# Eight of the 22 up-projection pairs of a ConvFFN computed as seven quarter products instead of eight, with the weight sums on GpSimd

## The chip, the cores and the metric

The kernel runs on one core of one Trainium2 chip. The metric is device microseconds of one execution, and the number for a kernel is the median over its runs. Five engines work side by side, each through its own queue of instructions in order: TensorE (PE in the profile) multiplies matrices, VectorE (DVE), ScalarE (ACT) and GpSimd (POOL) do elementwise work, and SyncE (SP) issues transfers; GpSimd issues some transfers as well. An instruction that waits for another engine holds back all that stands behind it in its own queue.

## The reference

One decoder layer on 512 tokens of width 1024: three token mixers, a gated merge, an output projection, and then the part that the change touches, a gated feed-forward net with a causal convolution over time:

```python
h = rmsnorm(x, norm_ffn_pre)                  # 512 x 1024
u = h @ ffn_w_up                              # 512 x 5632: gate and value halves
u = causal_conv3(u) + b                       # depthwise, over time
y = gelu_tanh(u[:, :2816]) * u[:, 2816:]      # 512 x 2816
x = x + rmsnorm(y @ ffn_w_down, norm_ffn_post)
```

The names in these lines are shortened; the arithmetic is float32.

## The kernel before

**Precision.** Every float32 operand of a matmul is split in two: `hi`, a rounded copy in TensorE's float32 format (made by ScalarE), and `lo`, the rest (a subtraction on VectorE). A product is then three matmuls, hi·hi, lo·hi and hi·lo, added up in PSUM. `mm3` (lines 112 to 114) issues them for the projections. `split` (lines 70 and 71) makes the hi and lo of a weight tile: one cast of 128x1024 on ScalarE, one subtraction of 128x1024 on VectorE.

**Weights of the up-projection.** `ffn_w_up` lies in memory as 44 tiles of 128x1024, one tile for each 128 output channels: eight blocks of 128 columns, one for each 128 of the 1024 input channels. Tile 2n is the gate half of pair n and tile 2n+1 its value half, so there are 22 pairs. `load_raw` loads a tile (line 66, on SP's queue, two buffers tagged `raw`), `split` makes `whi` and `wlo` (four buffers each), and `weight` keeps two tiles ahead of the one in use.

**The up stage.** The normalised tokens stand transposed as `h2h` and `h2l` (eight blocks of 128 channels by 512 tokens). For each tile the eight blocks are multiplied and added up in one PSUM tile of 128 channels x 512 tokens: 8 x 3 = 24 matmuls of 128x512, 48 for a pair. Pairs 0 and 1 (`FIRST`) are done as two halves of 256 tokens each while the tokens are still being made. `conv` (lines 838 to 841) is one ScalarE pass and two VectorE passes over the PSUM tile, and `up_finish` applies GELU (line 853), multiplies the halves of the pair (lines 855 and 863) and prepares operands for the down stage: even pairs make `y7` and one part of `ay`, odd pairs three sums in `ay` (lines 856 to 867, 128x256 each, on VectorE).

**The down stage** is already made of seven products where the plain way takes eight: tokens, output columns and the 22 input blocks are halved, and `steps` lists for each of the seven the left operand (a sum of halves of y) and the weight quarter that is added to or loaded into the chain of weights. `chain_load` (lines 879 to 886) does that with transfers: SP's queue loads a quarter, GpSimd's queue (line 884) adds one in flight. `l_split` (lines 933 and 934) makes hi and lo of a left operand, four blocks at a time, in two `lhs` buffers; step 0 takes `y7`, which is ready made. `q_mm` (lines 963 to 965) issues 462 matmuls of 128x512 in all.

**What sets the order.** The program is written in the order of its stages, and a scheduler places each engine's instructions; on TensorE the order is that of the program. Buffers with tags go round, so an early load waits until the last reader of its buffer is done.

Of the kernel before, what the change touches and what calls it, by code (L numbers as in the profile page):

```python
# [52 lines left out]
def kernel(ctx: ExitStack, tc: tile.TileContext, x, xT, w_first, w_tiles, w_v, w_br, w_out, w_up, w_down,  # L53
# [776 lines left out]
    with tc.tile_pool(name="fp", bufs=1) as fp:  # L830
        y7 = fp.tile([P, 2, NH, TH], F32R, tag="y7", name="y7")
        a2 = fp.tile([P, 2, NH, TH], F32, tag="a2", name="a2")
        ay = fp.tile([P, 4, NH, TH], F32, tag="ay", name="ay")
# [11 lines left out]
        kept = {}  # L845

        def up_finish(n, pg, pv):

# [4 lines left out]
            nc.scalar.activation(tg, tg, AF.Gelu_apprx_tanh)
            if n % 2 == 0:
                nc.vector.tensor_mul(tg, tg, tv)
                nc.vector.tensor_sub(tv[:, :TH], tg[:, TH:], tg[:, :TH])
                nc.scalar.copy(y7[:, 0, i, :], tv[:, :TH])
                nc.scalar.copy(ay[:, 2, i, :], tg[:, :TH])
                nc.vector.tensor_sub(y7[:, 1, i, :], tv[:, :TH], y7[:, 0, i, :].bitcast(F32))
                kept[i] = tg  # L860
            else:
# [1 line left out]
                nc.vector.tensor_mul(a2[:, :, i, :], tg.rearrange("p (h t) -> p h t", h=2),
                                     tv.rearrange("p (h t) -> p h t", h=2))
# [2 lines left out]
                nc.vector.tensor_sub(ay[:, 3, i, :], a2[:, 0, i, :], ay[:, 1, i, :])
# [262 lines left out]
```

## Time and profile before

| | us |
|---|---|
| median of 3 runs (lowest to highest) | 779.81 (779.64 to 779.97) |
| the profiled execution, its own time | 779.64 |
| span of the profile | 777.9 |
| up stage, matmuls from 423.8 to 666.5 | 242.7 |
| of this pairs 2 to 21, from 448.85 to 666.47 | 217.6 |
| down stage, from 666.5 to the last matmul's start at 771.0 | 104.5 |

The profile is of one execution. Its span starts with the first instruction and ends with the last; 1.7 us of the execution's own time lie around it. The granted clock of TensorE was 0.999 of full speed. A row of a group names the line of the kernel, the engine and the operation, `out<-in` by the program's names without buffer numbers, the shape and the count; behind the bar stand busy time, mean ns of one, and the idle time of the engine just before. A row of the timeline begins with start and duration. Matmuls overlap: the next starts before the last has ended, so the distance between two starts, not the duration, tells what one costs.

### The profile page before, as it was taken

What the parts mean: (1) busy time and instruction counts of PE and PEld (TensorE: products, weight loads), DVE (VectorE), ACT (ScalarE), POOL (GpSimd) and SP (SyncE); (2) the same over time, 40 slices, a digit from 0 to 9 for tenths busy, and PEclk for the clock granted to TensorE, in tenths of its full rate; (3) what the DMA queues carried; (4) which work ended last, traced back from release to release, by engine and by line L of the source; (5) the groups of instructions that cost most, each with busy time, mean ns of one, the idle gap of its engine ahead of it and who ended that gap; (6) DMA issues with size and microseconds to landing.
All of it is one profiled execution on the core that took longest, in us unless ns stands there. A gap on an engine that the chain in (4) does not pass through costs nothing.

```text
span 777.9 us, 9728 instructions
## 1 busy us (share of the span) xinstructions
PE 769.8 (99%) x3686; PEld 639.0 (82%) x3686; DVE 514.6 (66%) x784; ACT 357.0 (46%) x583; POOL 55.7 (7%) x70
## 2 busy tenths in 40 slices
PE   9999999999999999999999999999999999999996
PEld 7899776888887887888888988888888888888885
DVE  5564678378696557654748557766666666766896
ACT  6554554482223342432535434434444343565582
POOL 0100000002503000000000100000000000233000
PEclk9999999999999999999999999999999999999999
DMA  8524212123134222232461473332322325499761
GB/s 308 189 94 146 71 56 81 55 82 109 54 98 133 82 81 72 92 109 81 136 217 54 142 211 109 109 108 82 110 90 100 107 83 136 130 187 194 195 214 54
DMA packets 28527, 92.56 MB, mean 119 GB/s; under 512 B 3393, under 2 KB 3665, under 8 KB 28481
## 3 DMA queue, kind: packets, MB, share of 16 engines
q1 hardware_dynamic: 24048, 77.83, 29.8%
q0 software_dynamic: 4288, 14.11, 9.2%
q8 instruction: 29, 0.48, 0.2%
q14 instruction: 18, 0.14, 0.1%
q10 hardware_dynamic: 144, 0.00, 0.0%
HBM read 89.84 MB, written 2.10 MB: 118 GB/s over the span
## 4 chain that ended last, share of the span: by engine, by line
PE 98%; DVE 0%; DMA 0%; issue 0%; ACT 0%; DVEq 0%
PE up L113 10%; PE up L114 10%; PE up L112 10%; PE pj L112 9%; PE pj L113 9%; PE pj L114 9%; PE q L965 4%; PE q L964 4%; PE q L963 4%; PE py L114 3%; PE py L113 3%; PE py L112 3%; PE pq L206 3%; PE pz L752 2%; PE pz L750 2%; PE pz L751 2%
## 5 line engine op out<-in xcount | busy, mean ns | idle before, releaser
L71 DVE TENSOR_TENSOR wlo<-raw,whi 128x1024 fp32r<-128x1024 f32 (+1 forms) x105 | 125.4, 1196 | 110.7 <-ACT whi L70 110.4
L70 ACT CAST whi<-raw 128x1024 fp32r<-128x1024 f32 (+1 forms) x105 | 107.4, 1025 | 184.4 <-PE pj L113 92.5
L112 PE MATMUL up<-h_hi,whi 128*128 128x512 f32 (+1 forms) x384 | 143.8, 375 | 0.0
L113 PE MATMUL up<-h_lo,whi 128*128 128x512 f32 (+1 forms) x384 | 142.8, 372 | 0.0
L114 PE MATMUL up<-h_hi,wlo 128*128 128x512 f32 (+1 forms) x384 | 142.5, 371 | 0.0
L112 PE MATMUL pj<-h_hi,whi 128*128 128x512 f32 x296 | 120.8, 408 | 0.0
L113 PE MATMUL pj<-h_lo,whi 128*128 128x512 f32 x296 | 116.1, 392 | 0.0
L114 PE MATMUL pj<-h_hi,wlo 128*128 128x512 f32 x296 | 115.8, 391 | 0.0
L113 PEld LDWEIGHTS up<-h_lo,whi 128*128 128x128 f32 x384 | 72.3, 188 | 12.6
L114 PEld LDWEIGHTS up<-h_hi,wlo 128*128 128x128 f32 x384 | 72.3, 188 | 12.5
L112 PEld LDWEIGHTS up<-h_hi,whi 128*128 128x128 f32 x384 | 72.2, 188 | 12.3
L112 PEld LDWEIGHTS pj<-h_hi,whi 128*128 128x128 f32 x296 | 55.7, 188 | 16.2 <-issue 3.4
L114 PEld LDWEIGHTS pj<-h_hi,wlo 128*128 128x128 f32 x296 | 55.6, 188 | 12.0 <-issue 0.2
L113 PEld LDWEIGHTS pj<-h_lo,whi 128*128 128x128 f32 x296 | 55.8, 188 | 10.7 <-issue 1.2
L71 DVE TENSOR_TENSOR wlo<-chain,whi 128x1024 fp32r<-128x1024 f32 (+1 forms) x42 | 47.3, 1131 | 20.0 <-ACT whi L70 20.0
L70 ACT CAST whi<-chain 128x1024 fp32r<-128x1024 f32 (+1 forms) x42 | 41.2, 981 | 29.6 <-PE q L965 22.7
L884 POOL DMA_DIRECT2D chain<-in_w_down_dram x24 | 21.1, 878 | 435.1 <-DMA chain<-in_w_down_dram 200.0
L963 PE MATMUL q<-whi,lhs 128*128 128x512 f32 x132 | 51.3, 389 | 0.0
L964 PE MATMUL q<-wlo,lhs 128*128 128x512 f32 x132 | 51.3, 389 | 0.0
L965 PE MATMUL q<-whi,lhs 128*128 128x512 f32 x132 | 51.3, 389 | 0.0
L675 DVE TENSOR_TENSOR g<-pj,rstd_b 128x512 f32<-128x512 f32 x24 | 16.4, 687 | 27.3 <-PE pj L114 27.3
L963 PEld LDWEIGHTS q<-whi,lhs 128*128 128x128 f32 x132 | 24.8, 188 | 5.2
(308 smaller groups left out, 1264.8 us busy)
## 6 DMA issues: line engine op xcount, KB each, us to landing
raw<-in_w_up_dram SPq DMA_DIRECT2D x44, 512.0 KB, 3.3
raw<-in_w_tiles_dram SPq DMA_DIRECT2D x37, 512.0 KB, 3.3
chain<-in_w_down_dram SPq DMA_DIRECT2D x20, 512.0 KB, 4.5
chain<-in_w_down_dram POOLq DMA_DIRECT2D x20, 512.0 KB, 6.9
raw<-in_w_br_dram SPq DMA_DIRECT2D x12, 512.0 KB, 3.3
raw<-in_w_out_dram SPq DMA_DIRECT2D x8, 512.0 KB, 3.3
raw<-in_w_v_dram SPq DMA_DIRECT2D x8, 328.0 KB, 3.0
xT<-in_xT_dram SPq DMA_DIRECT2D x8, 256.0 KB, 5.1
```

What stands on the lines that cost most here:

```text
L70: nc.scalar.copy(hi[:, c], raw[:, c])
L71: nc.vector.tensor_sub(lo[:, c], raw[:, c], hi[:, c].bitcast(F32))
L112: nc.tensor.matmul(ps, lh, rh, start=first, stop=False)
L113: nc.tensor.matmul(ps, lh, rl, start=False, stop=False)
L114: nc.tensor.matmul(ps, ll, rh, start=False, stop=last)
L206: nc.tensor.matmul(pq[i], w[:, kc, i * P : (i + 1) * P], h[:, kc, :], start=kc == 0 and n == 0, stop=kc == KC - 1 and n == 2)
L675: nc.vector.tensor_mul(g1, gates.pop((br, m)), rstd_b)
L750: nc.tensor.matmul(pz[t][n], mh[:, kc % 4, tk], wh[:, ns], start=kc == 0, stop=False)
L884: nc.gpsimd.dma_start(c, w_down[kh, nh, :, k, :], accum_op=ALU.add)
L963: nc.tensor.matmul(ps, hi, wh[:, c], start=k == 0 and not last, stop=False, skip_group_check=last)
L964: nc.tensor.matmul(ps, hi, wl[:, c], start=False, stop=False, skip_group_check=last)
L965: nc.tensor.matmul(ps, lo, wh[:, c], start=False, stop=k == NH - 1, skip_group_check=last)
```

## The change

`SEVEN` lists eight pairs, 5, 7, ... 19. Each is done together with the plain pair behind it.

For such a pair the gate tile and the value tile are taken as one matrix with four quarters: b11 and b21 are the gate tile's columns for the first and the second half of the input channels, b12 and b22 those of the value tile. The tokens are halved too. Seven products of quarters (each 4 blocks x 3 = 12 matmuls of 128 channels x 256 tokens, line 1047) take the place of the eight plain ones: 84 matmuls of 128x256 for 48 of 128x512. Four of the seven take sums of quarters of the tokens as moving operand: `ys[0]` to `ys[3]`, made once by `y_steps` on VectorE and ScalarE during pairs 2 to 4, in five parts. Four take sums of weight quarters: `p3 = b12 + b22`, `p2 = b11 + p3`, `p1 = b11 + b12`, `p4 = b21 + p2`, added by GpSimd (lines 927 to 929 and 948) from two raw tiles `sra` and `srb` that `s_load` loads while the pair before is in work. `half` splits a quarter of 128x512 into hi and lo.

TensorE's order for two pairs n and n+1 is: b11, b21, p3, six matmuls of the plain tile 2n+2, p2, nine of it, p1, nine of it, p4, b22, and then the 24 of tile 2n+3. p2, p1 and b22 add to the PSUM tile `bx` in which b11 stands. `keep` copies the state of it between them to SBUF on ScalarE (`q1`, `nv`, `u`, and `n7` of p3), since the next product writes over it. Three VectorE operations (lines 1078, 1091, 1092) and one copy (line 1094) put the gate's and the value's result together in `ua` and `ub`, and `up_finish` goes on from SBUF.

The ring of weights is now made of half tiles (`slots`), in the same four buffers; `fill` prepares as many items ahead as fit.

`up_finish` writes one tensor `act`; of the sums for the down stage it makes one per pair, on GpSimd (lines 902 and 904), and the others are made by `l_split` in the down stage, in place, on VectorE (lines 1021 and 1023). Step 0 of the down stage has no ready operand any more, so `l_split` runs for it as well. The `lhs` buffers lie where `ys[2]` and `ys[3]` were, and four of the six chain buffers where `ys[0]` and `ys[1]` were, so that the chain loads follow the last of the eight pairs.

```diff
+SEVEN = (5, 7, 9, 11, 13, 15, 17, 19)
...
-        y7 = fp.tile([P, 2, NH, TH], F32R, tag="y7", name="y7")
-        a2 = fp.tile([P, 2, NH, TH], F32, tag="a2", name="a2")
-        ay = fp.tile([P, 4, NH, TH], F32, tag="ay", name="ay")
-        ch = [fp.tile([P, 2 * T], F32, tag=f"ch{p}", name=f"chain{p}") for p in range(4)]
+        act = fp.tile([P, 5, NH, TH], F32, tag="act", name="act")
+        wt = [new_w() for _ in range(4)]
...
+            whole(t1, 0, 1)
+            whole(t2, 1, 1)
+            nc.vector.tensor_sub(t2, t2, t1)
+            yield
+            parts(2, t2)
...
             if n % 2 == 0:
-                nc.vector.tensor_mul(tg, tg, tv)
-                nc.vector.tensor_sub(tv[:, :TH], tg[:, TH:], tg[:, :TH])
-                nc.scalar.copy(y7[:, 0, i, :], tv[:, :TH])
-                nc.scalar.copy(ay[:, 2, i, :], tg[:, :TH])
-                nc.vector.tensor_sub(y7[:, 1, i, :], tv[:, :TH], y7[:, 0, i, :].bitcast(F32))
-                kept[i] = tg
+                nc.gpsimd.tensor_sub(act[:, 4, i, :], act[:, 1, i, :], act[:, 0, i, :])
             else:
-                t0 = kept.pop(i)
-                nc.vector.tensor_mul(a2[:, :, i, :], tg.rearrange("p (h t) -> p h t", h=2),
-                                     tv.rearrange("p (h t) -> p h t", h=2))
-                nc.vector.tensor_sub(ay[:, 0, i, :], t0[:, TH:], a2[:, 1, i, :])
-                nc.vector.tensor_sub(ay[:, 1, i, :], t0[:, :TH], ay[:, 0, i, :])
-                nc.vector.tensor_sub(ay[:, 3, i, :], a2[:, 0, i, :], ay[:, 1, i, :])
+                nc.gpsimd.tensor_sub(act[:, 1, i, :], act[:, 1, i, :], act[:, 3, i, :])
...
+            for j, g in enumerate(("sra", "srb")):
+                qt[g] = f4(f"{g}{n}", g)
+                nc.sync.dma_start(qt[g], w_up[2 * n + j])
+            a, b = qt["sra"], qt["srb"]
...
+            nc.gpsimd.tensor_add(qt["p3"], b[:, :T], b[:, T:])
+            nc.gpsimd.tensor_add(qt["p2"], a[:, :T], qt["p3"])
+            nc.gpsimd.tensor_add(qt["p1"], a[:, :T], b[:, :T])
...
+            if q == "b21":
+                r = half(a[:, T:])
+                nc.gpsimd.tensor_add(a[:, T:], a[:, T:], qt["p2"])
+                return r
+            if q == "b22":
+                r = half(b[:, T:])
+                later = [m for m in SEVEN if m > n]
+                if later:
+                    s_load(later[0])
+                return r
...
+            quarter(bx, "b11", hq(0, 0), True)
+            q1 = keep("q1", bx)
+            quarter(bz, "b21", hq(1, 0), True)
+            nc.vector.tensor_add(ua[:, :TH], bz[:, :TH], q1)
+            quarter(by, "p3", yq(0), True)
+            n7 = keep("n7", by)
+            w = up_weight("t", 2 * n + 2)
+            whole_mm(pn[0], w, range(0, 2))
+            quarter(bx, "p2", yq(1), False)
+            nv = keep("nv", bx)
+            whole_mm(pn[0], w, range(2, 5))
+            quarter(bx, "p1", yq(2), False)
+            u = keep("u", bx, -1.0)
+            whole_mm(pn[0], w, range(5, 8))
...
+            quarter(by, "p4", hq(1, 1), False)
+            nc.vector.tensor_add(ua[:, TH:], by[:, :TH], nv)
+            nc.vector.tensor_sub(ub[:, TH:], u, n7)
+            quarter(bx, "b22", yq(3), False)
+            nc.scalar.activation(ub[:, :TH], bx[:, :TH], AF.Copy, scale=-1.0)
+            up_finish(n, ua, ub)
+            whole_mm(pn[1], up_weight("t", 2 * n + 3), range(KC))
...
+            if s == 3:
+                nc.vector.tensor_sub(src, src, act[:, 1, k0:k1, :])
+            if s == 5:
+                nc.vector.tensor_sub(src, act[:, 2, k0:k1, :], act[:, 0, k0:k1, :])
```

**How the order of the engines moves.** ScalarE in the up stage, before: the casts of two pairs' four weight tiles (line 70) with the work of `up_finish` between them.

```order
L70 CAST whi_4713<-raw_4711 128x1024
L838 ACTIVATE t0_4698<-up26_4642,small_sb_86 128x512
L853 ACTIVATE t0_4698<-t0_4698 128x512
L70 CAST whi_4744<-raw_4742 128x1024
L838 ACTIVATE t0_4702<-up27_4673,small_sb_86 128x512
L70 CAST whi_4789<-raw_4787 128x1024
L838 ACTIVATE tk_4773<-up28_4717,small_sb_86 128x512
L853 ACTIVATE tk_4773<-tk_4773 128x512
L70 CAST whi_4820<-raw_4818 128x1024
```

ScalarE now, from the first copy of pair 15 on (line 1068 is `keep`, line 933 the cast in `half`, line 941 the cast of a whole tile, names that end in `_15` and `_17` belong to these pairs):

```order
L1068 ACTIVATE q1_5091<-ux_15_5068 128x256
L933 CAST whi_3664<-sra15_4904 128x512
L933 CAST whi_3664<-srb15_4906 128x512
L941 CAST whi_3666<-raw_5134 128x1024
L1068 ACTIVATE n7_5132<-uy_15_5069 128x256
L1068 ACTIVATE nv_5156<-ux_15_5068 128x256
L933 CAST whi_3668<-sra17_5110 128x512
L933 CAST whi_3670<-p3_17_5116 128x512
L1068 ACTIVATE u_5179<-ux_15_5068 128x256
L933 CAST whi_3668<-sra17_5110 128x512
L884 ACTIVATE t0_5224<-ua_15_5073,small_sb_86 128x512
```

The copy `u` of pair 15 now stands behind two casts for pair 17, and these read what a load (`sra17`) and a GpSimd sum of a second load (`p3_17`) bring.

VectorE at the same place, before, for one pair:

```order
L71 TENSOR_TENSOR wlo_4714<-raw_4711,whi_4713 128x1024
L839 SCALAR_TENSOR_TENSOR t0_4698<-up26_4642,small_sb_86,t0_4698 128x511
L841 SCALAR_TENSOR_TENSOR t0_4698<-up26_4642,small_sb_86,t0_4698 128x510
L71 TENSOR_TENSOR wlo_4745<-raw_4742,whi_4744 128x1024
L839 SCALAR_TENSOR_TENSOR t0_4702<-up27_4673,small_sb_86,t0_4702 128x511
L841 SCALAR_TENSOR_TENSOR t0_4702<-up27_4673,small_sb_86,t0_4702 128x510
L863 TENSOR_TENSOR a2_3676<-t0_4698,t0_4702 128x2x256
L865 TENSOR_TENSOR ay_3677<-tk_4622,a2_3676 128x256
L866 TENSOR_TENSOR ay_3677<-tk_4622,ay_3677 128x256
L867 TENSOR_TENSOR ay_3677<-a2_3676,ay_3677 128x256
```

VectorE now, from the product of pair 15's halves to the last subtraction of pair 17's weights (lines 934 and 942 are the subtractions for quarters and whole tiles):

```order
L899 TENSOR_TENSOR act_3663<-t0_5224,t0_5228 128x2x256
L887 SCALAR_TENSOR_TENSOR t0_5263<-up32_5071,small_sb_86,t0_5263 128x510
L934 TENSOR_TENSOR wlo_3667<-p2_17_5115,whi_3666 128x512
L934 TENSOR_TENSOR wlo_3667<-p1_17_5114,whi_3666 128x512
L885 SCALAR_TENSOR_TENSOR t0_5267<-up33_5072,small_sb_86,t0_5267 128x511
L934 TENSOR_TENSOR wlo_3669<-sra17_5110,whi_3668 128x512
L887 SCALAR_TENSOR_TENSOR t0_5267<-up33_5072,small_sb_86,t0_5267 128x510
L1078 TENSOR_TENSOR ua_17_5279<-uz_17_5276,q1_5297 128x256
L899 TENSOR_TENSOR act_3663<-t0_5263,t0_5267 128x2x256
L934 TENSOR_TENSOR wlo_3669<-srb17_5112,whi_3668 128x512
L942 TENSOR_TENSOR wlo_3671<-raw_5340,whi_3670 128x1024
```

The three sums of 128x256 per pair have gone from here to GpSimd and into the down stage; the subtraction on `srb17`, after which the buffer `srb` may be loaded for pair 19, stands next to last in this stretch, behind two convolutions.

ScalarE at the end of the up stage, now, in pair 19 and the tiles 42 and 43 of pair 21 (`raw_5592`, `raw_5596`; `chain01` is a chain buffer of the down stage, line 1024 the cast in `l_split`):

```order
L1068 ACTIVATE u_5581<-ux_19_5480 128x256
L941 CAST whi_3670<-raw_5596 128x1024
L1024 CAST lhs2_5733<-act_3663 128x1024
L941 CAST whi_3668<-raw_5592 128x1024
L71 CAST whi_3664<-chain01_5673 128x1024
L1094 ACTIVATE ub_19_5486<-ux_19_5480 128x256
L884 ACTIVATE t0_5627<-ua_19_5485,small_sb_86 128x512
L884 ACTIVATE t0_5631<-ub_19_5486,small_sb_86 128x512
```

Before, the chains were loaded at the start of the up stage, and each chain's cast stood behind the convolution of the tile whose buffer it took; now the cast of the first chain stands ahead of pair 19's last copy out of PSUM.

More of the change, by code (lines that the diff above doesn't have):

```diff
@@ new lines, in half, with prep @@
+        def half(src):
+            hi, lo = slots(1)
+            nc.scalar.copy(hi, src)
+            nc.vector.tensor_sub(lo, src, hi.bitcast(F32))
+            return hi, lo
+        def prep(item):
+            if item[0] == "t":
+                hi, lo = slots(2)
+                raw = load_raw(w_up[item[1]])
+                nc.scalar.copy(hi, raw)
+                nc.vector.tensor_sub(lo, raw, hi.bitcast(F32))
+                return hi, lo
+            n, q = item[1:]
+            a, b = qt["sra"], qt["srb"]
+            if q == "b21":
[8 more added lines that the diff above has]
+                return r
+            return half(a[:, :T] if q == "b11" else a[:, T:] if q == "p4" else qt[q])
@@ new lines, with fill, up_weight @@
+        place = {}
+        def fill():
+            while done["i"] < len(items):
+                it = items[done["i"]]
+                size = 2 if it[0] == "t" else 1
+                at = slot["n"] + (size == 2 and slot["n"] % 2)
+                if at + size - min(place.values(), default=at) > 8 or (it[0] == "s" and not qt):
+                    break
+                place[it] = at
+                got_w[it] = prep(it)
+                done["i"] += 1
+        def up_weight(*item):
+            assert items[done["taken"]] == item, (items[done["taken"]], item)
+            done["taken"] += 1
+            fill()
+            return got_w[item]
@@ L873, with free @@
+        def free(*item):
+            del place[item]
+        steps = ((act[:, 4], (1, 1), True), (act[:, 0], (0, 0), False), (act[:, 1], (0, 1), True),
+                 (act[:, 0], (1, 1), True), (act[:, 3], (1, 0), True), (act[:, 1], (1, 1), False),
+                 (act[:, 2], (1, 0), False))
         pairs = tuple((k, min(k + 2, NH)) for k in range(0, NH, 2))
@@ L941, in l_prepare, with whole_mm, part_mm @@
                 l_split(*lgroups[len(left)])
+        def whole_mm(ps, w, kcs):
+            hi, lo = w
+            for kc in kcs:
+                c = slice(kc * P, (kc + 1) * P)
+                mm3(ps, hi[:, c], lo[:, c], h2h[:, kc, :], h2l[:, kc, :], kc == 0, kc == KC - 1)
+        def part_mm(ps, w, r, first):
+            for kc in range(4):
+                c = slice(kc * P, (kc + 1) * P)
+                terms = ((w[0], r[0]), (w[0], r[1]), (w[1], r[0]))
+                for t, (x, y) in enumerate(terms):
+                    nc.tensor.matmul(ps[:, :TH], x[:, c], y[:, kc, :], start=first and kc == 0 and t == 0,
+                                     stop=kc == 3 and t == 2, skip_group_check=not first)
```

155 lines of the change are left out of this document (114 added, 41 removed).

## The prediction

> **What bounds the kernel now.** First the page: the busy shares and the chain of waits that ended last.
>
> ```profile
> PE 769.8 (99%) x3686; PEld 639.0 (82%) x3686; DVE 514.6 (66%) x784; ACT 357.0 (46%) x583; POOL 55.7 (7%) x70
> ...
> PE 98%; DVE 0%; DMA 0%; issue 0%; ACT 0%; DVEq 0%
> ```
>
> TensorE is the path, and nothing else has 1% of it. So a change pays what it takes off TensorE's stream, and costs what makes that stream wait. The second view is the matmuls' timeline in the up stage, for the distance from start to start:
>
> ```profile
> 439.01 0.28 PE L114 MATMUL up<-h_hi,wlo 128*128 128x256 f32 x1
> ...
> 448.85 0.40 PE L112 MATMUL up<-h_hi,whi 128*128 128x512 f32 x1
> ...
> 666.47 0.39 PE L963 MATMUL q<-whi,y 128*128 128x512 f32 x1
> ```
>
> From 448.85 to 666.47 run 20 pairs of 48 matmuls: 217.62 us / 960 = 0.2267 us each, with no wait anywhere. From 439.01 to 448.85 run 82 of half the width: 9.84 / 82 = 0.1200 us each, across several changes of tile. A half costs 53% of a whole. The third view is the stretches, columns us, then busy us and instructions of PE, PEld, DVE, ACT, POOL:
>
> ```profile
> core 0: us, PE busy (x) PEld busy (x) DVE busy (x) ACT busy (x) POOL busy (x), PEclk, DMA share, GB/s
> 449.00:471.00 22.00, 22.00 (x99) 18.19 (x98) 12.83 (x18) 8.40 (x13) 0.00 (x0) 1.00 0.69 193
> 471.00:493.00 22.00, 22.00 (x99) 18.22 (x98) 16.30 (x23) 10.49 (x15) 0.00 (x0) 1.00 0.29 96
> ...
> 581.00:603.00 22.00, 22.00 (x98) 18.21 (x97) 14.30 (x20) 9.14 (x13) 0.00 (x0) 1.00 0.29 96
> ...
> 666.30:681.30 15.00, 15.00 (x68) 12.43 (x67) 11.04 (x13) 8.34 (x10) 5.12 (x4) 1.00 0.53 143
> 741.20:756.20 15.00, 15.00 (x68) 12.43 (x67) 15.00 (x28) 12.47 (x20) 0.00 (x0) 1.00 0.69 211
> ```
>
> VectorE is about two thirds busy in the up stage, and GpSimd idle. In the last row VectorE is busy all the time and TensorE still never waits: work queued far enough ahead hides.
>
> **TensorE.** A plain pair costs 48 x 0.2267 = 10.88 us, a pair of seven products 84 x 0.1200 = 10.08 us. That is 0.80 us for each of eight pairs, 6.4 us, if the halves run as at 439 and nothing waits. The down stage has the same 462 matmuls.
>
> The distance depends on the operands, which move to other places. Rows with three others:
>
> ```profile
> L751 PE MATMUL pz<-wlo,mg_hi 128*128 128x512 f32 x32 | 12.7, 397 | 0.0
> L114 PE MATMUL py<-y_swa_hi,wlo 128*128 128x512 f32 x32 | 12.6, 394 | 0.0
> L751 PE MATMUL pz<-wo_lo,mg_hi 128*128 128x512 f32 x24 | 9.4, 390 | 0.0
> L206 PE MATMUL pq<-h_hi,w_lo 128*128 128x512 f32 x32 | 8.6, 389 | 0.0
> ...
> 377.77 0.40 PE L750 MATMUL pz<-whi,mg_hi 128*128 128x512 f32 x1
> ...
> 396.21 0.40 PE L751 MATMUL pz<-wlo,mg_hi 128*128 128x512 f32 x1
> ```
>
> The slow ones stand 0.2334 us apart (79 in 18.44 us), 6.7 ns more. In the compiled program the tiles of the slow rows start at different bytes modulo 128 (weights 64; `mg`, `y_swa` 0), those of the fast rows at the same (64 and 64, or 0 and 0). Near or far in the memory does not sort them: `w_lo` lies far from `h_hi`, and its row is fast. After the change `ys`, the `lhs` buffers, the tokens and the weights all start at 64, so I take the fast distance. The dear end is 6.7 ns on 4 x 12 x 8 = 384 matmuls with `ys` and on 462 with `lhs`: 2.6 + 3.1 = 5.7 us.
>
> **VectorE and ScalarE per two pairs** (21.76 us of TensorE before, 10.08 + 10.88 = 20.96 after):
>
> ```profile
> L71 DVE TENSOR_TENSOR wlo<-raw,whi 128x1024 fp32r<-128x1024 f32 x97 | 118.8, 1226 | 101.8 <-ACT whi L70 101.7
> L841 DVE SCALAR_TENSOR_TENSOR t<-up,small_sb,t 128x510 f32<-128x510 f32 x33 | 24.7, 748 | 1.1
> L863 DVE TENSOR_TENSOR a<-t,t 128x512 f32<-128x512 f32 x11 | 7.6, 691 | 0.3
> L71 DVE TENSOR_TENSOR wlo<-chain,whi 128x512 fp32r<-128x512 f32 x7 | 4.8, 684 | 0.0
> L867 DVE TENSOR_TENSOR ay<-a,ay 128x256 f32<-128x256 f32 x11 | 4.7, 425 | 0.4
> ...
> L70 ACT CAST whi<-raw 128x1024 fp32r<-128x1024 f32 x97 | 101.6, 1049 | 173.0 <-PE pj L113 91.1 <-PE up L113 39.5 <-DMA raw<-in_w_up_dram 17.3
> L838 ACT ACTIVATE t<-up,small_sb 128x512 f32<-128x512 f32 x33 | 25.6, 775 | 0.0
> L853 ACT ACTIVATE t<-t 128x512 f32<-128x512 f32 x11 | 7.0, 632 | 21.5 <-DVE t L841 21.5
> L396 ACT COPY s<-sc 128x256 f32<-128x256 f32 x16 | 5.1, 374 | 0.2
> L70 ACT CAST whi<-chain 128x512 fp32r<-128x512 f32 x7 | 4.4, 622 | 1.4 <-PE q L965 1.1
> ```
>
> VectorE before: 4 x 1.23 + 8 x 0.75 + 2 x 0.69 + 5 x 0.43 = 14.4 us. After: 2 x 1.23 + 7 x 0.68 + 8 x 0.75 + 2 x 0.69 + 3 x 0.43 = 15.9 us of 20.96. ScalarE after: 2 x 1.05 + 7 x 0.62 + 4 x 0.78 + 2 x 0.63 + 5 x 0.37 = 12.7 us. Neither is full; what counts is the latest wait.
>
> **The latest wait** in a period, with 0 at b11's first matmul: p1 ends at 10.6, p4 at 14.1, and there b22 writes over `bx`, which `u` must have copied. ScalarE's order puts the casts on `sra` and `p3` of the next pair ahead of `u`. `srb` may be loaded when VectorE has done the subtraction on b22. VectorE gets to it after a run of work that starts behind p4: one convolution pass of ScalarE (0.8), then 3 subtractions of a quarter, one of a tile, the eight convolution passes, two products and two operations of 128x256, with the b22 one itself, 12.2 us by the rows above and less than 1 us of them waiting. That ends at 14.3 + 0.8 + 12.2 = 27.3, which is 6.3 of the next period. Then load, sum, cast, copy:
>
> ```profile
> raw<-in_w_up_dram SPq DMA_DIRECT2D x44, 512.0 KB, 3.3
> ...
> chain<-in_w_down_dram SPq DMA_DIRECT2D x20, 512.0 KB, 4.5
> ```
> ```profile
> 181.26 1.89 POOL L313 TENSOR_TENSOR s<-u 128x512 f32<-128x512 f32 x1 [20.12 <-DVE u L308]
> ...
> 191.20 1.04 POOL L313 TENSOR_TENSOR s<-s 128x512 f32<-128x512 f32 x1
> ```
> ```profile
> 236.18 3.13 POOL L737 TENSOR_SCALAR g_mix_post<-g_mix_post 128x1024 f32<-128x1024 f32 x1 [3.32 <-DMA g_mix_post<-in_g_mix_post_dram]
> ```
> ```profile
> 181.03 1.22 DVE L71 TENSOR_TENSOR wlo<-raw,whi 128x1024 fp32r<-128x1024 f32 x1
> ...
> 237.18 1.47 DVE L71 TENSOR_TENSOR wlo<-raw,whi 128x1024 fp32r<-128x1024 f32 x1
> ```
>
> 6.3 + 3.3 + 1.0 + 0.6 + 0.4 = 11.6 us, 2.4 ahead of 14.1. With the dear ends (4.5 for a load among others, 1.9 for a sum) it is 13.7, still in time. The other copies have more: `nv` can go at p2's end, 7.1, and is needed at 9.2. So I take no wait here.
>
> GpSimd and VectorE hinder each other where both read SBUF: the sum that starts at 181.26 beside VectorE's subtraction of 181.03 takes 1.89 us instead of 1.04, while VectorE's keeps its 1.22. At 237.18, beside GpSimd's work from 236.18 on, VectorE took 1.47. If VectorE lost all that GpSimd works in a period, 4 x 1.04 for the sums and 2 x 0.6 (estimated from half of 1.04) for the differences, 5.4 us, it would have 21.3 us to do in 20.96: 0.34 us in each of eight periods, 2.7 us. I take nothing, since the rows of 181 show GpSimd losing. The Trainium skill ("SBUF — State Buffer", section "SBUF: two separate sides") says that the two share one pair of ports under an exclusive lock, and that the later one fully blocks, so that by it both could lose, and the sum would be 773.5 + 2.7 = 776.2 at its worst; in the rows of 181 the one that starts later does lose.
>
> **The start.** `y_steps` adds 12 operations of 128x1024 to VectorE, near 1.23 us each, 14.8 us, by p3 of pair 5, 32.6 + 2.9 = 35.5 us behind 448.85. VectorE has 22 - 12.83 = 9.2 us free in the first stretch and 5.7 x 13.5 / 22 = 3.5 in the part of the second, and the sums that leave it free 5 x 0.43 / 2 a pair, 3.2 for three: 15.9. It fits, and narrowly; tile weights stand ahead of the sums where they are due. One sum also stands ahead of the last of the tokens' `lo` parts near 438 us, and TensorE has four more matmuls of ready tokens there. I take 0.1 us for both, from 0 to 2.
>
> **The end.** The chain loads move from the start of the up stage to pair 19, beside the last tiles' loads. What such a crowd costs shows where it is now, in the issues between 436 and 450 us:
>
> ```profile
> chain<-in_w_down_dram POOLq DMA_DIRECT2D x4, 512.0 KB, 12.6
> raw<-in_w_up_dram SPq DMA_DIRECT2D x2, 512.0 KB, 9.1
> ```
>
> Tile 43's load then goes out at 7.5 of pair 19's period and lands at 16.6; casts of 1.05 of it, of a left operand and of tile 42 end near 19.8, VectorE's three subtractions near 21.4, and TensorE wants tile 42's `lo` at 21.4. Nothing is left over: I take 0.2 us, from 0 to 1.5. The first chain, added in flight by 9 + 12.6 = 21.6, is due at 31.8 with about 7 us of work between. In the down stage the sums in place add 4 x 1.23 + 2 x 0.95 = 6.8 us of VectorE (the last two, of 128x768, estimated at three quarters) over several steps of 15 us, of which the first has 4.0 us free; nothing.
>
> **Sum.** 779.64 - 6.4 + 0.1 + 0.2 = 773.5 us against the profiled execution's own time; the median of the runs is 0.17 above it, and I leave the forecast at 773.5. A measurement of this kernel can tell about 0.2%, 1.6 us, from no change.
>
> **The rivals.** *The slow distance.* `ys` and `lhs` fall among the slow operands, by a rule of place that I read wrongly: 773.5 + 5.7 = 779.2 us, no change. Against it: the fast rows sort by the start modulo 128 without an exception. Half of it, `ys` or `lhs` alone, gives 776.1 to 776.6. 0.10 for the whole.
>
> *A late `srb` (the other side).* The chain above has 2.4 us to spare, about 2 with the signals between engines. Were VectorE held by GpSimd's two differences in its run (1.2), slowed as at 237.18 in two or three subtractions (0.25 each, 0.6), the load 1.2 and the sum 0.85 longer, it would come 3.9 late, 1.9 over. TensorE would then wait 1.9 us at b22 in seven periods: 773.5 + 13.3 = 786.8 us, slower. It decides at 6.4 / 7 = 0.9 us of wait, so at 2.9 us of delay. For it: the rows of 237.18 and the full VectorE; against it: loads one after the other landed in 3.3 us at every place in the up stage but its crowded start, and VectorE idles about 3 us between the subtractions that the loads release. 0.17.
>
> *The halves cost more than at 439*, for want of weights loaded in time between quarters: the gain is gone at 10.88 / 84 = 0.1295 us. The 82 in a row speak against it; this goes into the small cases, 0.05, with no change.
>
> *Small waits* of 0.2 to 0.5 us in a period, as by GpSimd's 0.34, or a crowd at the end that costs 2 us: 775 to 777.5. 0.10.
>
> **How the numbers follow.** The forecast has 0.58, small waits 0.10 (both faster): 0.68. The slow distance 0.10 and the dearer halves 0.05, less 0.02 for the part of them that ends outside: same 0.13. The late `srb` 0.17 and that 0.02: slower 0.19. Low end: start and end at nothing, 773.2, less 0.4, the spread of the three runs (0.33) and a little: 772.8. High end: it takes in small waits and the slow distance, 780.0, and leaves out the late `srb`.
>
> **What would show it.** Right: 84 x 8 = 672 matmuls of line 1047 with 0.120 us between starts, 512-wide ones of the up and the down stage still at 0.2267, and a period of 20.96 us from one pair's b11 to the next's. Wrong: idle time of TensorE ahead of `ux` released by ScalarE's `u` (the late `srb`), 0.127 between starts on `ys` or 0.233 in the down stage (the slow distance), or a gap at tile 42.

## The result, and the profile after

The changed kernel takes 774.44 us (median of 4 runs, 774.36 to 775.14), the kernel before beside it on the same chip 779.89 (779.64 to 780.4). The ratio is 0.9931, with a 95% interval of 0.9914 to 0.9949: 5.4 us faster, where 6.1 were forecast. The profiled execution took 774.49 us, its span 772.6, at a granted clock of 0.998. The kernel before, run again beside the experiments on three chips, took 779.85 to 780.12 us, so a difference between two of the runs below is uncertain by some 0.3 us.

The page of the changed kernel, busy shares and the chain that ended last:

```profile
PE 764.5 (99%) x3974; PEld 647.9 (84%) x3974; DVE 561.2 (73%) x814; ACT 384.4 (50%) x648; POOL 128.6 (17%) x124
...
PE 98%; DVE 0%; DMA 0%; issue 0%; ACT 0%; DVEq 0%
```

TensorE is still the path. At the head of TensorE's wait list stands the start of the program; its only other row is 0.2 us in the mixer, and none is of the up stage:

```profile
PE warm L183 <- POOL ones L167: 1.0, 1, 1.0
```

So in the up stage TensorE waits for nothing, as forecast. Its timeline, where the stage's parts begin (first column the start):

```profile
449.07 0.40 PE L113 MATMUL up<-h_hi,whi 128*128 128x512 f32 x1
...
481.74 0.28 PE L1047 MATMUL ux<-h_hi,whi 128*128 128x256 f32 x1
...
502.77 0.28 PE L1047 MATMUL ux<-h_hi,whi 128*128 128x256 f32 x1
...
516.91 0.28 PE L1047 MATMUL ux<-ys,whi 128*128 128x256 f32 x1
...
518.35 0.40 PE L113 MATMUL up<-h_hi,whi 128*128 128x512 f32 x1
...
523.82 0.28 PE L1047 MATMUL ux<-h_hi,whi 128*128 128x256 f32 x1
...
629.01 0.28 PE L1047 MATMUL ux<-h_hi,whi 128*128 128x256 f32 x1
644.59 0.40 PE L113 MATMUL up<-h_hi,whi 128*128 128x512 f32 x1
...
660.94 0.39 PE L1154 MATMUL q<-whi,lhs 128*128 128x512 f32 x1
```

Pairs 2 to 21 take 660.94 - 449.07 = 211.87 us, before 217.62: 5.75 us came from here. From 502.77 to 629.01 lie six periods of two pairs, 126.24 / 6 = 21.04 us each, where 20.96 was forecast. The tiles 41 to 43, 72 matmuls from 644.59, go at 16.35 / 72 = 0.2271 with no gap at tile 42. The left operands of the down stage are read at the fast distance: its matmuls' rows have 389 ns, as before, and the stage takes 104.5 us as before.

```profile
L1154 PE MATMUL q<-whi,lhs 128*128 128x512 f32 x154 | 59.9, 389 | 0.0
...
L1047 PE MATMUL ux<-ys,whi 128*128 128x256 f32 x192 | 35.5, 283 | 0.0
```

What the path doesn't show is VectorE and GpSimd. One period of GpSimd's timeline and of VectorE's (start, duration; in brackets idle time before and what ended it):

```profile
511.69 1.29 POOL L927 TENSOR_TENSOR p<-srb 128x512 f32<-128x512 f32 x1 [1.54 <-DMA srb<-in_w_up_dram]
512.94 1.74 POOL L929 TENSOR_TENSOR p<-sra,srb 128x512 f32<-128x512 f32 x1
514.64 1.74 POOL L928 TENSOR_TENSOR p<-sra,p 128x512 f32<-128x512 f32 x1
```
```profile
511.93 1.61 DVE L934 TENSOR_TENSOR wlo<-sra,whi 128x512 fp32r<-128x512 f32 x1 [2.38 <-ACT whi L933]
513.67 1.56 DVE L934 TENSOR_TENSOR wlo<-p,whi 128x512 fp32r<-128x512 f32 x1
515.15 1.51 DVE L1092 TENSOR_TENSOR ub<-u,n 128x256 f32<-128x256 f32 x1
516.59 0.68 DVE L934 TENSOR_TENSOR wlo<-sra,whi 128x512 fp32r<-128x512 f32 x1
```

Alone a subtraction takes 0.68 us (516.59), beside the sums 1.61 and 1.56. The ends alternate: 512.98 POOL, 513.54 DVE, 514.68 POOL, 515.23 DVE, 516.38 POOL, 516.66 DVE. VectorE's two subtractions of 128x512 end 0.55 us after the operation of GpSimd that ran into them, the one of 128x256 0.28 after it, and GpSimd's end 1.15 after VectorE's. So it looks as if one works while the other stands still. The Trainium skill ("SBUF — State Buffer", section "SBUF: two separate sides") says just this, that whichever starts first holds the shared ports for the whole instruction; the trace agrees here, and it isn't one engine alone that loses, as I had read from the rows of 181 us. In the prediction's row of 237.18 it doesn't agree: by the profile's spans GpSimd's operation there lasts until 239.31, and VectorE's subtraction, which started 1.0 us later, was done at 238.65.

### The profile page after: what moved, and what is told of

Same layout as the page of the kernel before. It is cut to its first block, busy times and chain, and to the rows that moved or that the text cites. A ratio compares the mean times of both kernels' runs of the same rounds, so it can differ in the third digit from the quotient of the medians.

```text
span 772.6 us, 10489 instructions
## 1 busy us (share of the span) xinstructions
PE 764.5 (99%) x3974; PEld 647.9 (84%) x3974; DVE 561.2 (73%) x814; ACT 384.4 (50%) x648; POOL 128.6 (17%) x124
## 4 chain that ended last, share of the span: by engine, by line
PE 98%; DVE 0%; DMA 0%; issue 0%; ACT 0%; DVEq 0%
PE pj L113 9%; PE pj L114 9%; PE pj L115 9%; PE up L114 7%; PE up L113 7%; PE up L115 7%; PE ux L1047 6%; PE q L1154 5%; PE q L1156 5%; PE q L1155 5%; PE uy L1047 3%; PE py L115 3%; PE py L114 3%; PE py L113 3%; PE pq L207 3%; PE pz L753 2%
## 5 line engine op out<-in xcount | busy, mean ns | idle before, releaser
L71 ACT CAST whi<-raw 128x1024 fp32r<-128x1024 f32 (+1 forms) x65 | 65.4, 1009 | 135.4 <-PE pj L114 92.6
L72 DVE TENSOR_TENSOR wlo<-raw,whi 128x1024 fp32r<-128x1024 f32 (+1 forms) x65 | 76.3, 1178 | 51.2 <-ACT whi L71 51.1
L113 PE MATMUL up<-h_hi,whi 128*128 128x512 f32 (+1 forms) x256 | 94.3, 370 | 0.0
L114 PE MATMUL up<-h_lo,whi 128*128 128x512 f32 (+1 forms) x256 | 93.4, 365 | 0.0
L115 PE MATMUL up<-h_hi,wlo 128*128 128x512 f32 (+1 forms) x256 | 92.7, 362 | 0.0
L1154 PE MATMUL q<-whi,lhs 128*128 128x512 f32 x154 | 59.9, 389 | 0.0
L1156 PE MATMUL q<-whi,lhs 128*128 128x512 f32 x154 | 59.9, 389 | 0.0
L115 PEld LDWEIGHTS up<-h_hi,wlo 128*128 128x128 f32 x256 | 48.3, 189 | 7.8
L113 PEld LDWEIGHTS up<-h_hi,whi 128*128 128x128 f32 x256 | 48.2, 189 | 6.6
L114 PEld LDWEIGHTS up<-h_lo,whi 128*128 128x128 f32 x256 | 48.4, 189 | 6.3
L942 DVE TENSOR_TENSOR wlo<-raw,whi 128x1024 fp32r<-128x1024 f32 x24 | 33.7, 1403 | 3.1 <-ACT whi L941 3.0
```

The lines of the kernel that those rows point to most:

```text
L71: nc.scalar.copy(hi[:, c], raw[:, c])
L72: nc.vector.tensor_sub(lo[:, c], raw[:, c], hi[:, c].bitcast(F32))
L113: nc.tensor.matmul(ps, lh, rh, start=first, stop=False)
L114: nc.tensor.matmul(ps, lh, rl, start=False, stop=False)
L115: nc.tensor.matmul(ps, ll, rh, start=False, stop=last)
L942: nc.vector.tensor_sub(lo, raw, hi.bitcast(F32))
```

## The experiments

**Where the operands begin.** Runs to test the rule of the prediction that a matmul is 6.7 ns dearer where its operands begin in different halves of 128 bytes. First, `ys` and with them the left operands moved by 64 bytes:

```diff
+        fp.tile([P, 16], F32, tag="shift", name="shift")
         ys = [fp.tile([P, 2, 4, TH], F32R, tag=f"ys{i}", name=f"ys{i}") for i in range(4)]
```

> The changed kernel with 64 unused bytes ahead of the ys buffers, so that ys and lhs, and only they of what TensorE reads, start at 0 modulo 128 while weights and tokens start at 64. Theory (the distance between matmuls is 6.7 ns more where the two operands start in different halves of 128 bytes): 384 quarter matmuls on ys at 0.1267 us instead of 0.1200, 2.6 us, and 462 of the down stage at 0.2334 instead of 0.2267, 3.1 us: 774.4 + 5.7 = 780.1 us. Rival (the slow rows of the first profile are slow because their operands lie far from each other, or by what runs beside them): nothing has moved but by 64 bytes, 774.4 us.

Measured: 777.62 us (777.01 to 777.99, 6 runs), ratio to the kernel before 0.997, 0.9958 to 0.9982. Its groups:

```profile
L1155 PE MATMUL q<-whi,lhs 128*128 128x512 f32 x154 | 60.9, 396 | 0.0
...
L1048 PE MATMUL ux<-ys,whi 128*128 128x256 f32 x192 | 35.1, 280 | 0.0
```

The down stage got dearer as expected: its rows went from 389 to 396 ns, and in the trace it takes 107.57 us instead of 104.49, 3.1 more, which is 462 x 6.7 ns. The quarters with `ys` did not: 280 ns, less than the 283 before, and 118.1 ns from start to start instead of 119.6. Half of the rule held. That the whole time also moved by 3.2 us (777.62 - 774.44) is partly chance: pairs 2 to 21 took 0.4 us less, and the stage ahead of them, which the edit leaves as it is, 0.6 us more.

Second, the other way round: pads that bring the mixer's operands, which are in different halves before and after the change, to the same half as their weights.

```diff
+    cp.tile([P, 16], F32, tag="shift", name="shift")
     ident = cp.tile([P, P], F32, tag="ident", name="ident")
...
-    cp.tile([P, 8], F32, tag="pad", name="pad")
+    cp.tile([P, 24], F32, tag="pad", name="pad")
...
-        mp.tile([P, 8], F32, tag="pad", name="pad")
+        mp.tile([P, 24], F32, tag="pad", name="pad")
```

> The changed kernel with pads that move the tiles of the mixer stage by 64 bytes, so that y_swa, y_pool, y_gla, mg, wo and ident start at 64 modulo 128 like the weights. Theory (start of the operands): the 288 matmuls py and the 96 matmuls pz on whi and wlo come down from 0.2334 to 0.2267 us each, 384 x 6.7 ns = 2.6 us, all else as it was: 774.4 - 2.6 = 771.8 us, faster than both kernels. Rival (place, or what runs beside): 774.4 us, with 394 and 397 ns in these rows as before.

Measured: 771.85 us (771.74 to 772.16, 4 runs), ratio 0.9897, 0.9882 to 0.9911. This is the fastest version; it beats both kernels. Its rows of `py` and `pz`, which the prediction shows at 394 and 397:

```profile
L115 PE MATMUL py<-y_swa_hi,wlo 128*128 128x512 f32 x32 | 12.5, 390 | 0.0
...
L753 PE MATMUL pz<-wlo,mg_hi 128*128 128x512 f32 x32 | 12.4, 389 | 0.0
```

The same pads in the kernel before:

> The kernel before with the same three pads that the mixer-aligned version has: what the mixer's matmuls read begins in the same half of 128 bytes as their weights; nothing else changes. Theory (the start of the operands alone sets 0.2334 against 0.2267 in the mixer, whatever the up stage does): 779.9 - 2.6 = 777.3. Rival (the gain came from a shift of what lies behind in SBUF, the quarters and their sums, and is only there with seven products): 779.9.

Measured: 777.24 us (776.9 to 777.41, 5 runs), ratio 0.9964, 0.9951 to 0.9977. The gain of 2.6 us (2.9 against the kernel before on the same chip, 780.12) is the mixer's own and has nothing to do with the change.

Third, with 256-wide matmuls spared when `ys` moved, all weights moved instead:

```diff
+    wp.tile([P, 16], F32, tag="shift", name="shift")
+    hp.tile([P, 16], F32, tag="shift", name="shift")
     def load_raw(src, cols=1024):
```

> All tile weights begin 64 bytes earlier modulo 128 (at 0 instead of 64); the tokens, ys and the left operands stay at 64, the mixer's other operands at 0. Theory (a 512-wide matmul takes 6.7 ns more where its moving and its stationary operand begin in different halves of 128 bytes; a 256-wide one takes nothing more): 888 of the mixer, 576 of up and 462 of down get dearer and 384 of the mixer (py, pz) cheaper, 1542 x 0.0067 = 10.3 us, so 784.8, up to 786 if the 192 of 328 columns get dearer too; the quarters of up stay at 0.120. Rival (the 256-wide ones with tokens or ys pay as well, and only the direction of the shift spared them when ys was moved): 864 x 0.0067 = 5.8 us more, 790.6, with the quarters at 0.127.

Measured: 776.02 us (773.12 to 776.44, 4 runs; why one was at 773.12 I don't know), ratio 0.9935, 0.9906 to 0.9963. Neither expectation held, 784.8 or 790.6. Groups, then the timeline of the up stage:

```profile
L1159 PE MATMUL q<-whi,lhs 128*128 128x512 f32 x154 | 60.7, 394 | 0.0
...
L1050 PE MATMUL ux<-ys,wlo 128*128 128x256 f32 x96 | 26.9, 280 | 0.0
...
L118 PE MATMUL py<-y_swa_hi,wlo 128*128 128x512 f32 x32 | 12.6, 392 | 0.0
...
L754 PE MATMUL pz<-whi,mg_hi 128*128 128x512 f32 x32 | 12.4, 389 | 0.0
```
```profile
448.40 0.39 PE L116 MATMUL up<-h_hi,whi 128*128 128x512 f32 x1
...
481.37 0.28 PE L1050 MATMUL ux<-h_hi,whi 128*128 128x256 f32 x1
...
502.25 0.28 PE L1050 MATMUL ux<-h_hi,whi 128*128 128x256 f32 x1
...
523.12 0.28 PE L1050 MATMUL ux<-h_hi,whi 128*128 128x256 f32 x1
```

`pz` got cheaper (0.2267 us from start to start) and the down stage dearer (107.57 us instead of 104.49), as the rule says. The rest did not follow it. `py`, whose operands now begin in the same half, at 0 and 0, came down from 0.2333 only to 0.2288 to 0.2303, where 64 and 64 gave 0.2264 to 0.2277 in the aligned version. The mixer should have cost 3.4 us more, with 888 matmuls dearer and 384 cheaper; the up stage's first matmul comes at 423.58 instead of 423.98. The 144 whole matmuls on the tokens from 448.40 stand (481.37 - 448.40) / 144 = 0.2290 us apart, 2.1 ns more than in the changed kernel, where the same 144 from 449.07 to 481.74 stand 0.2269 apart, and not 6.7 more. And with all its quarters in different halves a period takes 20.87 us, 0.17 less than 21.04: on average over seven periods its 84 quarters take 9.89 us instead of 10.05, 1.9 ns less each, while its 48 whole matmuls take 10.99 as in the changed kernel.

So the rule holds for `pz` and the down stage, in which the weights are the moving operand; there the traces of all four runs agree with it. In `py` 64 and 64 is fast and 0 and 64 slow, but 0 and 0 lies between; for the tokens the size is another, and for 256 columns the sign. What decides this stays open.

**The gain per pair.** Four pairs in place of eight:

```diff
-SEVEN = (5, 7, 9, 11, 13, 15, 17, 19)
+SEVEN = (13, 15, 17, 19)
```

> Four of the pairs are made of seven products instead of eight (13, 15, 17, 19); the others are plain. Theory (the gain is per pair, 21.76 - 21.04 = 0.72, and nothing is paid once): four pairs' gain is missing, 774.44 + 4 x 0.72 = 777.3. Rival (of the 0.9 us missing from the forecast a part is paid once, at the first seven-product pair or at the end, so that the eight pairs bring 0.80 each less a constant): 774.44 + 4 x 0.80 = 777.65; only the trace's periods tell these two apart, at 21.04 or 20.96.

Measured: 777.2 us (777.12 to 777.27, 5 runs), ratio 0.9962, 0.9949 to 0.9975. The first two of its periods:

```profile
568.63 0.28 PE L1047 MATMUL ux<-h_hi,whi 128*128 128x256 f32 x1
...
589.67 0.28 PE L1047 MATMUL ux<-h_hi,whi 128*128 128x256 f32 x1
```

21.04 us again, and 2.8 us lost with four pairs: the gain is 0.7 a pair, with nothing paid once. Pairs 2 to 21 took 217.62 us in the kernel before, 214.74 here and 211.87 in the changed kernel, so that the last four pairs brought 2.88 us and the first four 2.87.

**What a period has beyond 20.96.** In the changed kernel's timeline above the 24 whole matmuls behind b22 go from 518.35 to 523.82, 5.47 us, where 0.2267 each would make 5.44. The shorter pieces of 6, 9 and 9 take 1.39, 2.07 and 2.07 instead of 1.36, 2.04 and 2.04. To test whether it is the change of width, one more such change, as a fourth piece:

```diff
-            whole_mm(pn[0], w, range(0, 2))
+            whole_mm(pn[0], w, range(0, 1))
...
-            whole_mm(pn[0], w, range(2, 5))
+            whole_mm(pn[0], w, range(1, 3))
...
-            whole_mm(pn[0], w, range(5, 8))
-            free("t", 2 * n + 2)
+            whole_mm(pn[0], w, range(3, 6))
             quarter(by, "p4", hq(1, 1), False)
+            whole_mm(pn[0], w, range(6, 8))
+            free("t", 2 * n + 2)
```

> The plain tile between the quarters is cut into four pieces (3, 6, 9 and 6 matmuls, behind p3, p2, p1 and p4) instead of three (6, 9, 9), so there is one change more from quarters to whole tiles in a period. Theory (each change to 512 columns costs 0.02 to 0.03 us, which is what the period has beyond 20.96): the period is 21.06 instead of 21.04, and the total 774.6. Rival (the 0.08 us of a period are something else, as the plain tile's or the quarters' own distance): 21.04 and 774.44.

Measured: 780.41 us (778.1 to 782.82, 8 runs), ratio 1.0005, 0.9991 to 1.0019; the whole gain is gone. Its timeline and TensorE's waits:

```profile
502.70 0.28 PE L1047 MATMUL ux<-h_hi,whi 128*128 128x256 f32 x1
...
523.75 0.28 PE L1047 MATMUL ux<-h_hi,whi 128*128 128x256 f32 x1
```
```profile
PE ux L1047 <- ACT q L1068: 5.6, 4, 2.0
```

A period without a wait takes 21.05, between what the two expected, so the run doesn't settle it; each of its five pieces is again 0.02 to 0.03 us over. The kernel before has the same: its first 24 whole matmuls behind the halves of pairs 0 and 1, from 448.85, take 5.46 us, the next 24 take 5.44. So the surplus stands wherever whole matmuls follow halves, but no run parts the width from anything else that changes there. What cost most of the gain is a wait of 5.6 us that neither expected: p2 waits for ScalarE's copy `q1`. The scheduler had placed ScalarE's work in another order, and the copy stood late in its queue.

**How near the late wait is.** The same wait showed in two more runs, one meant to price the cover that the pieces of the plain tile give to ScalarE's copies, the other for the rival of the late `srb`. The plain tile in one piece behind p1:

```diff
-                items += [("s", n, "b11"), ("s", n, "b21"), ("s", n, "p3"), ("t", 2 * n + 2), ("s", n, "p2"),
-                          ("s", n, "p1"), ("s", n, "p4"), ("s", n, "b22"), ("t", 2 * n + 3)]
+                items += [("s", n, "b11"), ("s", n, "b21"), ("s", n, "p3"), ("s", n, "p2"),
+                          ("s", n, "p1"), ("t", 2 * n + 2), ("s", n, "p4"), ("s", n, "b22"), ("t", 2 * n + 3)]
...
             quarter(by, "p3", yq(0), True)
             n7 = keep("n7", by)
-            w = up_weight("t", 2 * n + 2)
-            whole_mm(pn[0], w, range(0, 2))
             quarter(bx, "p2", yq(1), False)
             nv = keep("nv", bx)
-            whole_mm(pn[0], w, range(2, 5))
             quarter(bx, "p1", yq(2), False)
             u = keep("u", bx, -1.0)
-            whole_mm(pn[0], w, range(5, 8))
+            w = up_weight("t", 2 * n + 2)
+            whole_mm(pn[0], w, range(KC))
```

> The changed kernel with the plain tile 2n+2 in one piece of 24 matmuls behind p1, instead of 6, 9 and 9 between the quarters. Theory (the pieces hide ScalarE's copies of the PSUM tile, and each change from 256 wide to 512 wide costs 0.02 us): p1 must now wait for nv, whose copy ends 0.6 to 0.7 us behind p2 in the trace, in each of eight periods, 5.2 us, and two changes of width less save 0.3 us: 774.4 + 4.9 = 779.3 us, with TensorE waiting for ScalarE's line 1068 eight times. Rival (the copies need no cover, the pieces only add changes of width): 774.1 us.

Measured: 785.77 us (784.4 to 787.17, 4 runs), ratio 1.0074, 1.0059 to 1.0089. And p3's sum issued four times:

```diff
-            nc.gpsimd.tensor_add(qt["p3"], b[:, :T], b[:, T:])
+            for _ in range(4):
+                nc.gpsimd.tensor_add(qt["p3"], b[:, :T], b[:, T:])
```

> The changed kernel with GpSimd's first sum, p3, done four times over, the result being the same. In the trace of the changed kernel the copy u ends 2.9 us ahead of the matmul that needs it, and one p3 sum takes 1.29 to 1.35 us. Theory (the latest wait of a period is srb, sum, cast, u): three more sums put u 3.9 to 4.1 us later, 1.0 to 1.2 us over, in seven periods, 7 to 8.4 us: 781.4 to 782.8 us, TensorE waiting at ux for ScalarE's line 1068. If VectorE is held up too by the longer GpSimd work, up to 1.4 us more in a period, to 792. Rival (that chain has more room, or another wait is the latest): 774.4 to 775 us.

Measured: 802.08 us, the median of four runs, of which three took 800.64 to 803.09 us and one 2715.54, for no cause that I know; ratio of the three 1.0281, 1.026 to 1.0301. TensorE's waits in the first and in the second of the two, and ScalarE's cast in the second:

```profile
PE ux L1047 <- ACT q L1068: 8.2, 6, 2.8
```
```profile
PE ux L1048 <- ACT q L1069: 15.3, 7, 3.2
```
```profile
524.37 0.62 ACT L934 CAST whi<-p 128x512 fp32r<-128x512 f32 x1 [9.59 <-POOL p L928]
```

Both took longer than either of their expectations (779.3 the one, 792 at most the other). In both the edit moved other things as well: in the one the scheduler put six matmuls of the plain tile ahead of p1, so that here TensorE's order is not that of the program; in the other it put p1's sum and `u` in another place. So neither prices the cover or the late sum by itself. The second loses more than the waits that are listed: behind them TensorE's granted clock was lower, 0.95 from 524 us to 690, where it was 1.00 from 482 to 524. What the second shows is the queue: ScalarE stands 9.59 us at one cast that waits for GpSimd, and the copy that TensorE wants next period stands behind it. A run with only one sum more, in which ScalarE's order stays:

```diff
             nc.gpsimd.tensor_add(qt["p3"], b[:, :T], b[:, T:])
+            nc.gpsimd.tensor_add(qt["p3"], b[:, :T], b[:, T:])
```

> The sum of the lower half's two blocks (p3) is issued twice; what is computed stays the same. GpSimd gets 1.0 to 1.35 us more per pair, and the second sum stands behind p1's sum, so p2's sum and all that hangs on it come that much later, while ScalarE's order is unchanged. Theory (a late sum costs only what goes beyond the spare time of the chain, 2.9 us at ux by the changed kernel's own trace): 774.4, up to 776 where the second sum runs beside VectorE's subtractions at 1.8 us; no wait of TensorE at ux. Rival (the four-times run: any lateness sits in ScalarE's in-order queue and comes out at q1): 1.0 to 1.35 us times 8 or more, 782 to 785, with waits of TensorE for q1.

Measured: 781.17 us (780.63 to 782.42, 10 runs), ratio 1.0017, 1.0007 to 1.0026; 6.7 more than the changed kernel, between the 776 at most of the one expectation and the 782 at least of the other. TensorE's waits, then the timelines of SP, GpSimd and ScalarE in the period that begins at 503.30:

```profile
PE ux L1048 <- ACT u L1069: 5.2, 7, 0.9
```
```profile
503.30 0.28 PE L1048 MATMUL ux<-h_hi,whi 128*128 128x256 f32 x1
```
```profile
508.02 0.33 SPq L923 DMA_DIRECT2D sra<-in_w_up_dram  x1
510.21 0.33 SPq L923 DMA_DIRECT2D srb<-in_w_up_dram  x1
```
```profile
513.62 1.29 POOL L927 TENSOR_TENSOR p<-srb 128x512 f32<-128x512 f32 x1 [1.71 <-DMA srb<-in_w_up_dram]
514.87 1.29 POOL L930 TENSOR_TENSOR p<-sra,srb 128x512 f32<-128x512 f32 x1
516.12 1.30 POOL L928 TENSOR_TENSOR p<-srb 128x512 f32<-128x512 f32 x1
```
```profile
517.45 0.62 ACT L934 CAST whi<-p 128x512 fp32r<-128x512 f32 x1 [5.03 <-POOL p L928]
517.98 0.38 ACT L1069 ACTIVATE u<-ux 128x256 f32<-128x256 f32 x1
```

In the changed kernel the load and the copy of the period that begins at 502.77:

```profile
508.44 0.33 SPq L923 DMA_DIRECT2D srb<-in_w_up_dram  x1
```
```profile
513.61 0.38 ACT L1068 ACTIVATE u<-ux 128x256 f32<-128x256 f32 x1
```

This is the prediction's rival: TensorE waits for `u` ahead of b22. With the sum twice the copy ends at 518.36 - 503.30 = 15.06 of the period; in the changed kernel it ended at 513.99 - 502.77 = 11.2, and TensorE came for it at b22's first matmul, 516.91 - 502.77 = 14.14. So the sum delayed it by 3.85 us and the price is 0.9 a period (the row of waits has 5.2 us for seven periods; the twelve matmuls behind each wait also took 1.53 us instead of 1.43). Of the 3.85, 2.5 are GpSimd's: the second sum stands behind p1's and starts 2.5 us after the first. The rest comes from the period before: `srb`'s load goes out at 6.9 of the period, where it went at 5.7 in the changed kernel, because VectorE, late at p3, is late at the subtraction on b22 that sets `srb` free. To test that return, the same kernel with 3.0 us less for VectorE (from pair 5 on the convolution lacks its tap two tokens back):

```diff
+            if i < 2 * SEVEN[0]:
                 nc.vector.scalar_tensor_tensor(out=t0[:, 2:], in0=ps[:, : T - 2], scalar=col(C_CW + i), in1=t0[:, 2:],
                                                op0=ALU.mult, op1=ALU.add)
```

> As with p3's sum twice, and from pair 5 on VectorE's second convolution pass (the tap two tokens back) is left out, so that the output lacks that tap: 4 x 0.75 = 3.0 us less of VectorE per period, all of it behind the late sum; GpSimd's sums and ScalarE's order stay. Theory (the loss with p3's sum twice is a ring: a late p3 makes VectorE's in-order queue late, so the subtraction on b22 that releases the next load of srb is 1.4 us later in every period, and the ring takes 21.98 us): the ring is 19 us long, VectorE catches up, the load of srb goes out at 5.5 us of the period or earlier, no wait at ux, 774.4. Rival (the two sums more on GpSimd by themselves, 2.6 us, are what TensorE waits for): the wait of 0.8 to 0.9 us per period stays, 780 to 781.

Measured: 779.27 us (778.85 to 780.32, 8 runs), ratio 0.9993, 0.9981 to 1.0004. TensorE's waits, SP and GpSimd in the period that begins at 503.46:

```profile
PE ux L1049 <- ACT u L1070: 3.8, 7, 0.7
```
```profile
503.46 0.28 PE L1049 MATMUL ux<-h_hi,whi 128*128 128x256 f32 x1
```
```profile
507.78 0.33 SPq L924 DMA_DIRECT2D sra<-in_w_up_dram  x1
508.92 0.33 SPq L924 DMA_DIRECT2D srb<-in_w_up_dram  x1
```
```profile
513.53 1.29 POOL L928 TENSOR_TENSOR p<-srb 128x512 f32<-128x512 f32 x1 [5.18 <-DMA srb<-in_w_up_dram]
```

The theory missed by 5 us and the rival was near. The load did go out earlier, at 5.5 instead of 6.9, so VectorE is in the ring as said. But the sum starts at 10.1 instead of 10.3: now `sra` and `srb` go out 1.1 us apart, and `srb` takes 4.6 us from issue to sum instead of 3.4. The median from issue to landing says the same, 4.5 us for `srb` against 3.4 with the sum twice, while `sra` has 3.3 and 3.2. So the lateness is bounded by two things in turn, VectorE's queue and the load of `srb`; taking from the first brought 1.9 us of the 6.7. That the load of `sra` close ahead is what makes `srb` slower is argued, not shown, and ScalarE's order was not quite the same in this run.

**GpSimd or VectorE.** The sums and differences moved to VectorE (six places, lines 902, 904, 927 to 929 and 948):

```diff
...
-            nc.gpsimd.tensor_add(qt["p3"], b[:, :T], b[:, T:])
+            nc.vector.tensor_add(qt["p3"], b[:, :T], b[:, T:])
...
```

> All sums of the weights' quarters and the differences of the quarters of act on VectorE instead of GpSimd. VectorE's busy time per period goes up by four sums and two differences, 4 x 0.69 + 2 x 0.43 = 3.6 us, from some 15.9 (without what it loses beside GpSimd) to 19.5 of 21.04. Theory (VectorE's waits for the loads, some 1.7 us a period, come on top in its in-order queue, so that it is as long as TensorE's period): 774.4 to 777. Rival one (the loss of both engines beside each other is gone, and with it the only cost; the sums are 0.69 instead of 1.3 to 1.8): 774.4 and nothing else, since TensorE waits for nothing either way. Rival two (VectorE's queue holds gelu and the subtractions behind a late load): 780 or more.

Measured: 774.51 us (774.14 to 774.8, 4 runs), ratio 0.9928, 0.9913 to 0.9943: the time of the changed kernel. The stretches of one period, with the changed kernel's first (busy us and instructions of PE, PEld, DVE, ACT, POOL):

```profile
502.77:523.82 21.05, 21.05 (x134) 19.08 (x133) 17.58 (x24) 11.84 (x21) 8.99 (x6) 1.00 0.29 101
```
```profile
502.77:523.82 21.05, 21.05 (x134) 19.09 (x133) 17.51 (x29) 11.52 (x20) 0.00 (x0) 1.00 0.32 98
```

With five instructions more VectorE is busy 17.51 us, against 17.58 with the sums on GpSimd. What VectorE gets rid of by giving the sums away it loses again by standing still beside them. TensorE waits in neither, so the time can't tell theory and rival one apart; rival two is out.

## Why the prediction was right, and where it wasn't

*TensorE, 0.80 us a pair.* Right in kind, 0.08 too much. The row of 82 halves at 439 us gave 0.1200, and the quarters run at 0.1196; 0.2267 holds inside a long run of whole matmuls. The term that was mis-sized is the period of 20.96: it measured 21.04, eight times 0.08 = 0.64 us. That is the 0.65 by which pairs 2 to 21 fell short (5.75 us of 6.4), and most of the 0.9 missing. By the pieces' lengths each of the four places where whole matmuls follow quarters costs 0.03, and the quarters give a few hundredths back. That the width itself is the cause was argued, not shown.

*The start, 0.1, and the end, 0.2.* From 423.98 to 449.07 the first pairs took 25.09 us, before 25.06; tile 42 shows no gap, and the down stage is the same to 0.01 us. So both terms were nothing. In their place the span ends 7.17 us behind the last matmul's start instead of 6.93, and the up stage starts 0.19 us later. The second is not the change's: in the runs whose code up to there is the same it starts anywhere from 423.80 to 424.59.

*The latest wait, 2.4 us to spare.* The place was right, and so was the size: `u` ends at 513.99 and b22 comes at 516.91, so 2.9 are spare, and the delay of 3.85 in the run with two sums cost the 0.9 that this leaves. What I hadn't seen is that a delay doesn't end with its period: it comes back through VectorE's queue and the next load. And another copy stands as near in other orders: `q1`, which three runs ran into.

*GpSimd beside VectorE, taken at nothing.* The result was right and the reason wrong. I read from the rows of 181 that GpSimd loses; in the changed kernel both do, and VectorE's subtractions on `p` take 0.97 us on average instead of 0.68:

```profile
L934 DVE TENSOR_TENSOR wlo<-p,whi 128x512 fp32r<-128x512 f32 x24 | 22.8, 971 | 2.7 <-ACT whi L933 1.7
```

It cost nothing because VectorE is still done in time: 17.6 of 21.05 us busy. The 21.3 us that I had for the worst case counted VectorE's own work as 15.9, adding up durations that overlap at their ends; with the sums on it and nothing lost, 3.6 us of its 17.5 are the sums and differences, which leaves 13.9.

*The slow distance, 0.10.* It didn't come, and the whole 5.7 us couldn't have: `ys` in the other half got cheaper. The 3.1 us of the left operands were real. That the fast rows sort by the start without an exception was true of the rows at hand; the run with all weights moved has exceptions. The forecast was safe from this because the tokens, the weights, `ys` and `lhs` all stayed at 64, where 512-wide matmuls are fast by the rule and by the runs.

## What to carry to other kernels

A stage that is bound by TensorE pays what is taken off its stream, and the distance between starts, read from a run of the same shape, priced the period here to 0.4% and the gain to a tenth; then look for the copy or wait with the least time to spare, since an edit that only reorders can use it up. Work given to an idle GpSimd isn't free for VectorE where both read SBUF: compare VectorE's busy time with and without it before calling it a relief. Check where in 128 bytes the operands of long runs of matmuls begin, and try the pad, since the rule that fits one stage may not fit the next.
